# A tiled softmax whose stores alternate between the DMA queues of Pool and ACT

## The chip, the cores and the metric

The kernel runs on one core of a Trainium2 chip. The metric is the device time of one execution in microseconds; for several runs the median is given.

## The reference

The input `x` has the shape 32 x 512 x 1024 in float32, and `temperature` is 0.5. The output is a softmax over the last axis:

```python
scaled = x / temperature
shifted = scaled - np.max(scaled, axis=-1, keepdims=True)
exp_x = np.exp(shifted)
return (exp_x / np.sum(exp_x, axis=-1, keepdims=True)).astype(np.float32)
```

This is 16384 independent rows of 1024 numbers, 67.1 MB in and 67.1 MB out.

## The kernel before

The rows are cut into 11 tiles. A tile has 128 partitions, and each partition holds several whole rows: 11 in the first tile, 12 in tiles 1 to 9, and 9 in the last, tile 10. The rows of a partition are contiguous in memory, so that one DMA moves a whole tile with one contiguous run for each partition. Within a tile the rows are worked on in groups, which `PASSES` gives: 4, 4 and 3 rows in the first tile, 6 and 6 in the others, 4, 3 and 2 in the last.

Four buffers hold tiles (`BUFS`), and everything is done in place. SP issues the loads (line 62): four at the start, and then the load of tile i+4 after the store of tile i has landed, since it goes into the same buffer. For a group, `maximum` lets DVE reduce each row to its maximum (line 71) and scale it to a bias (line 74); `exponential` lets ACT take the exponential of each row with that bias, with the row's sum as a by-product (line 80); `divide` lets DVE take the reciprocal of the sums (line 92) and multiply the rows by it (line 95 in one instruction for tiles 2, 3, 4 and 6, line 98 row by row for the others). When the last group of a tile has been divided, `store` issues one DMA for the whole tile (line 110). The first store is held back by a small copy on Pool (line 108) that waits for the load of tile 2.

The order is written out by hand. Each engine runs its instructions in the order in which the loop emits them. For each group the loop emits the maximum and the exponential, and after these the divide (and, for a tile's last group, the store) of the group before it. From tile 9 on (`ALONE`) the last group of the tile before is finished ahead of the new tile's first maximum, and in the last tile (`HELD`) all three maxima and exponentials come ahead of the three divides. So on ACT a store stands in one line with the exponentials, and on Pool there is nothing but the stores and the small copy.

A store goes through the DMA queue of the engine that issues it: `queue = nc.gpsimd if i < BY_POOL else nc.scalar` with `BY_POOL = 6`. Tiles 0 to 5 are stored by Pool, tiles 6 to 10 by ACT. A transfer on a queue is served after those ahead of it on the same queue; transfers on different queues share the 16 DMA engines.

Of the kernel before, what the change touches and what calls it, by code (L numbers as in the profile page):

```python
# [1 line left out]

# [4 lines left out]

PASSES = [[4, 4, 3]] + [[6, 6]] * 9 + [[4, 3, 2]]  # L10
BUFS = 4

WHOLE = (2, 3, 4, 6)


BY_POOL = 6

ALONE = 9

HELD = len(PASSES) - 1  # L20


@with_exitstack
def kernel(
    ctx: ExitStack,
    tc: tile.TileContext,
    x: bass.AP,
    temperature: bass.AP,
    out: bass.AP,
):  # L30
    nc = tc.nc
    f32 = mybir.dt.float32
    scale = 1.0 / float(temperature)
    extreme = mybir.AluOpType.max if scale > 0 else mybir.AluOpType.min

    P = 128
    xf = x.flatten_outer_dims()
    of = out.flatten_outer_dims()
    n, d = xf.shape
    rows = [sum(ks) for ks in PASSES]  # L40
    assert sum(rows) * P == n

    data = ctx.enter_context(tc.tile_pool(name="data", bufs=BUFS))
    stats = ctx.enter_context(tc.tile_pool(name="stats", bufs=4))


    groups = []
    for i, ks in enumerate(PASSES):
        for j, k in enumerate(ks):
            groups.append((i, sum(ks[:j]), k))  # L50

    def dram(t, i):
        block = t[P * sum(rows[:i]) : P * sum(rows[: i + 1]), :]
        return block.rearrange("(p k) d -> p k d", p=P, k=rows[i])

    tiles, small = [], []

    def load():
        i = len(tiles)
        if i < len(PASSES):  # L60
            xt = data.tile([P, rows[i], d], f32, name="xt")
            nc.sync.dma_start(out=xt, in_=dram(xf, i))  # L62
            tiles.append(xt)

    def maximum(g):
        i, a, k = groups[g]
        top, bias, sums, recip = (
            stats.tile([P, k], f32, name=name) for name in ("top", "bias", "sums", "recip")
        )
        small.append((bias, sums, recip))  # L70
        nc.vector.tensor_reduce(  # L71
            out=top, in_=tiles[i][:, a : a + k, :], axis=mybir.AxisListType.X, op=extreme
        )
        nc.vector.tensor_scalar_mul(bias, in0=top, scalar1=-scale)  # L74

    def exponential(g):
        i, a, k = groups[g]
        bias, sums, _ = small[g]
        for b in range(k):
            nc.scalar.activation(  # L80
                tiles[i][:, a + b, :],
                tiles[i][:, a + b, :],
                mybir.ActivationFunctionType.Exp,
                bias=bias[:, b : b + 1],
                scale=scale,
                accum_out=sums[:, b : b + 1],
            )

    def divide(g):
        i, a, k = groups[g]  # L90
        _, sums, recip = small[g]
        nc.vector.reciprocal(recip, sums)  # L92
        if i in WHOLE:
            xt = tiles[i][:, a : a + k, :]
            nc.vector.tensor_mul(xt, xt, recip.unsqueeze(2).to_broadcast([P, k, d]))  # L95
            return
        for b in range(k):
            nc.vector.tensor_scalar_mul(  # L98
                tiles[i][:, a + b, :], in0=tiles[i][:, a + b, :], scalar1=recip[:, b : b + 1]
            )  # L100

    def store(g):
        i, a, k = groups[g]
        if a + k == rows[i]:
            if i == 0:


                nc.gpsimd.tensor_copy(stats.tile([P, 1], f32, name="seen"), tiles[2][:, 0, 0:1])  # L108
            queue = nc.gpsimd if i < BY_POOL else nc.scalar
            queue.dma_start(out=dram(of, i), in_=tiles[i])  # L110
            load()

    with tc.manual_schedule():
        for _ in range(BUFS):
            load()
        waiting = []

        def finish():  # L120
            for g in waiting:
                divide(g)
                store(g)
            waiting.clear()

        for g, (i, a, k) in enumerate(groups):
            if i >= ALONE and a == 0:
                finish()
            maximum(g)
            exponential(g)  # L130
            if i < HELD:
                finish()
            waiting.append(g)
        finish()


# [1 line left out]
_INS = ['x', 'temperature']  # L138
_OUTS = [((32, 512, 1024), 'float32')]

_NUMBERS = {'temperature': 0.5}


# [26 lines left out]
```

## Time and profile before

| what | value |
|---|---|
| time, median of 3 runs | 317.35 us (317.19 to 318.64) |
| the profiled execution: its time, its span | 318.96 us, 317.2 us |
| DVE busy | 252.3 us (80%) |
| ACT busy | 148.3 us (47%) |
| Pool busy | 3.7 us (1%) |
| moved | 134.24 MB, mean 423 GB/s |

The span runs from the first instruction to the last event that the profile shows; about 1.8 us of the profiled execution lie around it. In the profile, L110 is line 110 of the kernel; `xt<-in_x_dram` is a load, `out_dram<-xt` a store. Names such as SPq, POOLq and ACTq are the instruction queues of the engines, which issue the DMAs. DMA queue q1 is that of SP, q0 that of Pool (software_dynamic) and q10 that of ACT. A row of a timeline gives the start, the duration, the engine, the line and the operation, and in brackets the idle time before it with what ended it. A row of a table by stretch gives the stretch, its length, the busy time and count of DVE, ACT and Pool, the clock, the DMA's busy share and its GB/s.

### The profile page before, as it was taken

The page shows a single profiled execution, that of the slowest core. Times are in us where ns is not written, and L with a number is a line of the kernel's source. Part 1 is how long each engine was busy: PE and PEld are TensorE (multiplying, and loading weights), DVE is VectorE, ACT ScalarE, POOL GpSimd, SP SyncE. Part 2 cuts the span into 40 slices and gives each one's busy share as a digit, 9 for nine tenths or more (in the row PEclk, how much of TensorE's full clock was granted, in tenths as well). Part 3 has the DMA queues.
Part 4 walks back from the last instruction along what each step waited for, and adds up shares of the span by engine and source line. Part 5 has one row for each costly group of instructions (what it writes and reads, how often), then busy time and mean ns, then how long its engine had stood idle before and what let it go on. Part 6 is the DMA issues. An engine that isn't in the chain of part 4 may idle for free. (4 is left out here: it accounts for less than half of the span.)

```text
span 317.2 us, 542 instructions
## 1 busy us (share of the span) xinstructions
DVE 252.3 (80%) x160; ACT 148.3 (47%) x257; POOL 3.7 (1%) x11
## 2 busy tenths in 40 slices
DVE  0099999999999799969949994997199689779900
ACT  0048477468174353807171770438035805916600
POOL 0000010000000000000000000000000000000000
DMA  9999999999999999999999999999999999999994
GB/s 364 401 459 397 459 434 377 417 439 438 440 403 465 428 409 471 410 440 440 403 471 415 415 477 397 446 441 409 465 421 409 471 418 431 442 414 459 421 432 181
DMA packets 3171, 134.24 MB, mean 423 GB/s; under 512 B 352, under 2 KB 352, under 8 KB 352
## 3 DMA queue, kind: packets, MB, share of 16 engines
q1 hardware_dynamic: 1584, 67.11, 49.5%
q0 software_dynamic: 864, 37.22, 27.1%
q10 hardware_dynamic: 720, 29.88, 21.8%
q14 instruction: 3, 0.02, 0.0%
HBM read 67.11 MB, written 67.11 MB: 423 GB/s over the span
## 5 line engine op out<-in xcount | busy, mean ns | idle before, releaser
L80 ACT ACTIVATE xt<-xt,bias 128x1024 f32<-128x1024 f32 x128 | 145.2, 1135 | 133.7 <-DVE bias L74 64.6
L71 DVE TENSOR_REDUCE top<-xt 128x6 f32<-128x6144 f32 (+3 forms) x24 | 140.1, 5837 | 40.7 <-DMA xt<-in_x_dram 40.7
L98 DVE TENSOR_SCALAR xt<-xt,recip 128x1024 f32<-128x1024 f32 x80 | 54.5, 748 | 0.6
L95 DVE TENSOR_TENSOR xt<-xt,recip 128x6144 f32<-128x6144 f32 x8 | 52.5, 6559 | 0.6 <-DVE recip L92 0.2
L80 ACT ACTIVATION_READ_ACCUMULATOR xt<-xt,bias 128x1 f32 x128 | 23.8, 186 | 0.0
L80 ACT ACT_TABLE_LOAD x1 | 1.3, 1283 | 16.7 <-DMA xt<-in_x_dram 16.7
L92 DVE RECIPROCAL recip<-sums 128x6 f32<-128x6 f32 (+3 forms) x24 | 4.3, 180 | 5.8 <-ACT xt L80 5.8
L110 POOL DMA_DIRECT2D out_dram<-xt x6 | 3.3, 554 | 129.0 <-ACT xt L80 83.8
L74 DVE TENSOR_SCALAR bias<-top 128x6 f32<-128x6 f32 (+3 forms) x24 | 4.1, 171 | 0.8
L108 POOL COPY seen<-xt 128x1 f32<-128x1 f32 x1 | 0.2, 183 | 45.3 <-DMA xt<-in_x_dram 45.3
L151 POOL MEMSET const-bfloat16-1.0<- 128x1 bf16 x1 | 0.1, 102 | 0.0
L151 POOL MEMSET const-uint8-127<- 128x1 uint8 x1 | 0.1, 102 | 0.0
L151 POOL MEMSET const-float32-0.0<- 128x1 f32 x1 | 0.1, 99 | 0.2 <-issue 0.2
L151 POOL MEMSET const-float32-1.0<- 128x1 f32 x1 | 0.1, 99 | 0.0
## 6 DMA issues: line engine op xcount, KB each, us to landing
xt<-in_x_dram SPq DMA_DIRECT2D x9, 6144.0 KB, 37.1
out_dram<-xt POOLq DMA_DIRECT2D x5, 6144.0 KB, 36.7
out_dram<-xt ACTq DMA_DIRECT2D x4, 6144.0 KB, 32.6
xt<-in_x_dram SPq DMA_DIRECT2D x1, 5632.0 KB, 15.8
out_dram<-xt POOLq DMA_DIRECT2D x1, 5632.0 KB, 28.5
xt<-in_x_dram SPq DMA_DIRECT2D x1, 4608.0 KB, 39.5
out_dram<-xt ACTq DMA_DIRECT2D x1, 4608.0 KB, 15.5
```

Source lines behind the costliest of these rows:

```text
L71: nc.vector.tensor_reduce(out=top, in_=tiles[i][:, a : a + k, :], axis=mybir.AxisListType.X, op=extreme)
L74: nc.vector.tensor_scalar_mul(bias, in0=top, scalar1=-scale)
L80: nc.scalar.activation(tiles[i][:, a + b, :], tiles[i][:, a + b, :], mybir.ActivationFunctionType.Exp, bias=bias[:, b : b + 1], scale=scal ...
L92: nc.vector.reciprocal(recip, sums)
L95: nc.vector.tensor_mul(xt, xt, recip.unsqueeze(2).to_broadcast([P, k, d]))
L98: nc.vector.tensor_scalar_mul(tiles[i][:, a + b, :], in0=tiles[i][:, a + b, :], scalar1=recip[:, b : b + 1])
L108: nc.gpsimd.tensor_copy(stats.tile([P, 1], f32, name="seen"), tiles[2][:, 0, 0:1])
L110: queue.dma_start(out=dram(of, i), in_=tiles[i])
L151: nc = _bacc.Bacc("TRN2", target_bir_lowering=False, num_devices=1)
```

## The change

The rule for the queue of a store is no longer a limit but a list. Tiles 0, 2, 4, 6, 8 and 9 are stored by Pool, tiles 1, 3, 5, 7 and 10 by ACT. Pool still issues six stores and ACT five. On ACT each store keeps the place of its tile in the emitted order: the store of tile 1 now stands among ACT's exponentials after those of tile 2's first group, and so on. DVE and SP run the same instructions as before in the same order.

```diff
-BY_POOL = 6
+BY_POOL = (0, 2, 4, 6, 8, 9)
...
-            queue = nc.gpsimd if i < BY_POOL else nc.scalar
+            queue = nc.gpsimd if i in BY_POOL else nc.scalar
             queue.dma_start(out=dram(of, i), in_=tiles[i])
             load()
```

## The prediction

> **What bounds the kernel now.** I read the slices of the span and the DMA queues first, since they say whether any engine but the DMA has something to win.
>
> ```profile
> DMA  9999999999999999999999999999999999999994
> q1 hardware_dynamic: 1584, 67.11, 49.5%
> q0 software_dynamic: 864, 37.22, 27.1%
> q10 hardware_dynamic: 720, 29.88, 21.8%
> HBM read 67.11 MB, written 67.11 MB: 423 GB/s over the span
> ```
>
> The DMA engines are busy in every slice but the last. q1 carries the loads that SP issues, q0 the stores of Pool, q10 those of ACT; together they fill 98.4% of sixteen engines. A megabyte costs the same from each: 0.218 x 317.2 us / 29.88 MB = 2.31 us on q10, 2.31 us on q0, 2.34 us on q1. So a 12-row tile (6144 KB, 6.29 MB) costs all engines 14.55 us, and the last one (4608 KB, 4.72 MB) 10.9 us. q1's 1584 packets are 11 loads of 144, or 9 on each engine: 8 of data and one small one that ends the transfer. A data packet of a 12-row tile thus costs its engine 14.55/8 = 1.82 us, one of the last tile 1.36 us.
>
> The order of work at the end comes from the chain that ended last, from the stores on ACT's queue in the timeline, and from one row of DVE that shows when tile 9's load landed. I call the store and load of tile i S(i) and L(i).
>
> ```profile
> 208.96 35.04 DMA out_dram<-xt
> ...
> 244.14 39.52 DMA xt<-in_x_dram
> ...
> 283.68 4.43 DVE top L71
> ...
> 299.31 0.75 DVE xt L98
> ```
>
> ```profile
> 239.38 0.34 ACTq L110 DMA_DIRECT2D out_dram<-xt  x1
> 257.30 0.34 ACTq L110 DMA_DIRECT2D out_dram<-xt  x1
> 283.18 0.34 ACTq L110 DMA_DIRECT2D out_dram<-xt  x1
> 300.76 0.34 ACTq L110 DMA_DIRECT2D out_dram<-xt  x1
> ```
>
> ```profile
> 258.30 6.55 DVE L71 TENSOR_REDUCE top<-xt 128x6 f32<-128x6144 f32 x1 [1.02 <-DMA xt<-in_x_dram]
> ```
>
> S(6) lands at 244.0 and frees the buffer for L(10), which lands at 283.66. Then DVE and ACT need 17.1 us until S(10) is issued at 300.76. The DMA stays busy through these 17 us only because stores are still queued. How long they last, the DMA issues say when asked for the stretches around 239, 257, 283 and 300 us (KB and us from issue to landing):
>
> ```profile
> out_dram<-xt ACTq DMA_DIRECT2D x1, 6144.0 KB, 31.6
> out_dram<-xt ACTq DMA_DIRECT2D x1, 6144.0 KB, 33.6
> out_dram<-xt ACTq DMA_DIRECT2D x1, 6144.0 KB, 22.2
> out_dram<-xt ACTq DMA_DIRECT2D x1, 4608.0 KB, 15.5
> ```
>
> S(7) lands at 271.0, S(8) at 290.9, S(9) at 305.4, S(10) at 316.3; 0.9 us later the span ends. S(9) lasts 305.4 - 300.8 = 4.6 us beyond the issue of S(10). That is all the cover the tail has.
>
> Last, how two queues share the engines. Between 232 and 254 us both a load and a store were always queued:
>
> ```profile
> q1 hardware_dynamic: 109, 4.72, 49.7%
> q10 hardware_dynamic: 111, 4.67, 49.1%
> ```
>
> They take equal turns, packet by packet. This reproduces the tail by hand. L(10) lies behind L(9) until 258.3; its 8 packets alternate with 8 of stores: 8 x (1.36 + 1.82) = 25.4 us, landing 283.7 (measured 283.66). S(7) lands at 271.0, 12.7 us after 258.3, or four turns of 3.18 us: S(7) has four packets left at 258.3. S(8) gets the other four turns, and its last four packets alone take 7.3 us: 291.0 (measured 290.9). S(9) then takes 14.55 us: 305.5 (measured 305.4), S(10) 10.9 us: 316.3 (measured 316.3).
>
> **The change, part by part.** No arithmetic changes and no byte more is moved; 11 stores stay 11.
>
> *Issue.* S(1), S(3), S(5) go from Pool to ACT, S(6), S(8), S(9) from ACT to Pool, so ACT still issues five stores (0.34 us each, 0.85 the first) and Pool six (0.53). Behind a store on ACT stands the next group's exponential, which needs a maximum that DVE runs after the divide the store waits for (6.55 us and a 0.17 us bias). ACT's wait and its 0.34 us lie under that; without the cover three stores would cost 1 us in all. On Pool only later stores are queued. Pool is slower to start: the timeline has DVE's next maximum at 150.84, just after the last divide, and Pool's issue at 151.47, against 239.26 and 239.38 on ACT. So S(6), S(8), S(9) are issued some 0.7 us later, counting the longer issue; each then stands beside queued transfers, which hides it: nothing. S(10), the one that nothing covers, stays on ACT.
>
> *Bytes.* All queues pay 2.31 to 2.34 us per MB, so nothing is won or lost by moving bytes from one to the other.
>
> *Order of service.* Here is the cost. On one queue S(7) and S(8) are served one after the other, and a load beside them gets every second turn. On two queues both are served at once, and the load gets a smaller share. No row of this trace shows a store on q0, a store on q10 and a load all queued at length: at the handover, S(6) is issued on q10 at 208.96 while q0 finishes S(5). The bounds are every second turn (no slip) and every third. I take every third, because q1 and q10 share by equal turns above and q1 and q0 do so too (4.03 MB on q0 beside 3.83 MB on q1 from 188.5 to 206.5 us).
>
> Suppose everything up to 258.3 us stays: S(7) has four packets left, S(8) is queued. Four rounds of three, 4 x (1.82 + 1.82 + 1.36) = 20.0 us, end at 278.3; S(7) is done, S(8) and L(10) have four packets each. Four rounds of two, 12.7 us, end at 291.0, where L(10) lands and S(8) is done. L(10) lands 7.3 us later than before. Only S(9) is left to cover the 17.1 us of arithmetic: it ends at 305.5 while S(10) is issued at 291.0 + 17.1 = 308.1. The 2.6 us between, and the start of a transfer on idle engines, is time in which nothing moves. That start lies between nothing and 2.3 us (L(0) landed 15.8 us after its issue for 13.5 us of data); I take 1.2, the middle, since part of L(0)'s excess belongs to the first packets of the run. The end is 308.1 + 1.2 + 10.9 = 320.2, against 316.3: 3.9 us later. The profiled execution has a span of 317.2 us in a time of 318.96; its span becomes 321.1. The three runs shown have a median of 317.35, and I add the 3.9 to it: **321.2 us**.
>
> In general, each S(7) packet left when S(8) starts costs L(10) 1.82 us, and about 3.4 us (4.6 less the 1.2) are free: the loss begins at two packets, and four are there now.
>
> *Upstream.* The same overlap occurs at each earlier pair (S(0) lands some 9 us after S(1) is issued), so early stores land later and loads wait longer for buffers. But L(9) and L(10) are issued well before the queue ahead of them is empty (L(10) at 244.1 behind an L(9) that lands at 258.3), and some queue always has work, so the engines lose nothing there. It moves the phase: as stores win turns from loads, later stores come later against their predecessors. Whether S(7) meets S(8) with three, four or five packets left is the largest doubt: 1.8 us for each.
>
> *A rule against it.* The Trainium skill, DMA: Bandwidth & Descriptors, section Rules for kernel authors, says of spreading transfers over issuing engines for bandwidth: "Doesn't help — they all run on the same 16 DMA engines and interleave". By it alone the sum would be zero, 317.35 us; the equal price per MB above agrees with it on bandwidth, while the tail depends on which transfer comes first. The same page, section Queues, rings and completion order, has each engine take turns between queue rows packet by packet; by this the share would be a third, and the sum the one above, though no run here has shown three queues.
>
> **The rivals.**
>
> *No loss.* The load keeps half the turns, or S(7) is nearly done when S(8) starts, or the early engines decide. For the last there is a row, the end of the span:
>
> ```profile
> 313.00:317.20 4.20, 0.00 (x0) 0.00 (x0) 0.00 (x0) 1.00 0.06 26
> ```
>
> Only 6% of the engines' time is used after 313: most are done there, and one laggard ends at 316.3. The others have some 3 us less to do; if L(10) no longer waits for a packet of the laggard, it lands up to 3.4 us earlier than I reckon and the loss shrinks to about 0.5 us. Time: 317.3 to 318.4. Against it: the laggard serves the same packets as before.
>
> *Faster.* The laggard's 316.3 - 313 is the only DMA time left to win beside the start. If another order of packets spares it, the end comes up to 2.6 us earlier: 314.8 us. This decides only if the tail also keeps its cover, two packets or fewer of overlap; nothing in the profile says the laggard's lag comes from the queue chosen.
>
> *Worse.* S(9) is issued at about 283 and stands behind S(8) on q0. If S(8) ends two packets before L(10), S(9) spends two turns beside L(10) instead of under the arithmetic: 3.6 us more, about 324.8.
>
> **How the numbers follow.** About 0.5% (1.6 us) is what a measurement of this kernel can tell from no change. The forecast has 0.72 (its own span 319.2 to 323.4, one packet less to one packet more and the start latency), no loss 0.18, faster 0.05, worse 0.05. So slower by over 0.5% is 0.77, within 0.5% 0.18, faster 0.05. The range takes in the no-loss case and the forecast's upper end: 317.2 to 323.4.
>
> **What would show it.** Right: S(7)'s time to landing grows from 31.6 to about 39 us, L(10)'s from 39.5 to about 47; S(8) and L(10) land within a packet or two of each other; S(10) takes 12 to 13 us instead of 15.5; the DMA share falls near zero for some 3 us before S(10)'s data, where it is full now; q0 and q10 both carry data between 258 and 275. Wrong: L(10) landing near 284 with the share full to the end, or an idle stretch of the DMA in the middle.

## The result and the profile after

The changed kernel takes 325.16 us (median of 5 runs, 324.98 to 325.33), the kernel before 317.84 us (5 runs, 317.19 to 318.64). The ratio is 1.023, with a 95% interval from 1.021 to 1.0251: slower by 7.3 us, where 3.9 were forecast. The profiled execution of the changed kernel has a span of 323.4 us in a time of 325.16, so its span is 6.2 us longer than that of before. The granted clock was 1.00 in every run of this case, and the ratios leave out runs that lie over 1.5% above the fastest of their kernel.

The page of the changed kernel, its DMA slices and queues:

```profile
DMA  9999999998989999998989999999999999999666
q1 hardware_dynamic: 1584, 67.11, 48.8%
q0 software_dynamic: 864, 37.22, 27.1%
q10 hardware_dynamic: 720, 29.88, 21.4%
```

The bytes on each queue are the same. What is new is at the end: the last three slices are busy to between six and seven tenths. DVE and ACT are busy for 252.3 and 148.3 us as before.

The stores of tiles 7, 8, 9 and 10 in the timeline of ACT and Pool:

```profile
236.95 0.34 ACTq L110 DMA_DIRECT2D out_dram<-xt  x1
255.20 0.53 POOL L110 DMA_DIRECT2D out_dram<-xt  x1 [42.20 <-DVE xt L98]
281.92 0.53 POOL L110 DMA_DIRECT2D out_dram<-xt  x1 [26.18 <-DVE xt L98]
310.19 0.34 ACTq L110 DMA_DIRECT2D out_dram<-xt  x1
```

The DMA issues in the stretches around 237, 255, 282 and 310 us (KB, and us from issue to landing):

```profile
out_dram<-xt ACTq DMA_DIRECT2D x1, 6144.0 KB, 40.8
out_dram<-xt POOLq DMA_DIRECT2D x1, 6144.0 KB, 38.1
out_dram<-xt POOLq DMA_DIRECT2D x1, 6144.0 KB, 25.7
out_dram<-xt ACTq DMA_DIRECT2D x1, 4608.0 KB, 12.3
```

S(7) takes 40.8 us instead of 31.6 and lands at 277.7; S(8) lands at 293.3, S(9) at 307.6, S(10) at 322.5. The chain that ended last has the load of tile 10 and the first instruction that waits for it; DVE's timeline has the first of tile 9 (start, duration, and in brackets the idle time before it):

```profile
249.17 43.91 DMA xt<-in_x_dram
293.10 4.43 DVE top L71
```

```profile
256.77 6.55 DVE L71 TENSOR_REDUCE top<-xt 128x6 f32<-128x6144 f32 x1 [1.86 <-DMA xt<-in_x_dram]
```

L(9) lands 1.5 us earlier than before, L(10) 9.4 us later, at 293.08. Then follow 17.1 us of arithmetic until S(10) is issued. The table by stretch (busy time of DVE, ACT and Pool, the clock, the DMA's busy share, GB/s) shows the DMA in the second half of them. A packet counts whole in the stretch in which it starts, so a share can also exceed 1.

```profile
303.00:306.00 3.00, 2.93 (x7) 3.00 (x7) 0.00 (x0) 1.00 0.38 164
306.00:309.00 3.00, 2.93 (x7) 2.11 (x4) 0.00 (x0) 1.00 0.00 0
```

From 306 to 309 us no packet of data starts. In the trace's packets the last one of S(9), begun before 306, ends at 307.3 us, and the first of S(10) starts at 311.0: for 3.7 us nothing moves. The cover that S(9) gave the tail is used up before the arithmetic is done.

### The profile page after: what moved, and what is told of

Read it like the earlier page. It is cut to its first block, busy times and chain, and to the rows that moved or that the text cites. A ratio compares the mean times of both kernels' runs of the same rounds, so it can differ in the third digit from the quotient of the medians.

```text
span 323.4 us, 542 instructions
## 1 busy us (share of the span) xinstructions
DVE 252.3 (78%) x160; ACT 148.3 (46%) x257; POOL 3.7 (1%) x11
## 3 DMA queue, kind: packets, MB, share of 16 engines
q1 hardware_dynamic: 1584, 67.11, 48.8%
HBM read 67.11 MB, written 67.11 MB: 415 GB/s over the span
## 4 chain that ended last, share of the span: by engine, by line
DMA 65%; DVE 26%; ACT 5%; issue 0%; DVEq 0%; SPq 0%; ACTq 0%
DMA xt<-in_x_dram 43%; DMA out_dram<-xt 21%; DVE top L71 18%; DVE xt L98 5%; ACT xt L80 5%; DVE xt L95 2%; DVE bias L74 1%; DVE recip L92 0%; DVEq L165 0%; SPq L62 0%; ACTq L80 0%
## 6 DMA issues: line engine op xcount, KB each, us to landing
out_dram<-xt POOLq DMA_DIRECT2D x5, 6144.0 KB, 35.2
xt<-in_x_dram SPq DMA_DIRECT2D x1, 4608.0 KB, 43.9
out_dram<-xt ACTq DMA_DIRECT2D x1, 4608.0 KB, 12.3
```

## How the loss came about: turns taken from the last load

The step that no row of before could show is in this trace. From 262.5 to 272.5 us S(7) on q10, S(8) on q0 and L(10) on q1 were all queued (packets, MB, share of the engines):

```profile
q10 hardware_dynamic: 32, 1.57, 36.3%
q0 software_dynamic: 30, 1.47, 35.5%
q1 hardware_dynamic: 33, 1.22, 28.6%
```

The three queues take equal turns, about two packets each on each of the 16 engines. L(10) gets every third turn, where it had every second beside a single store queue.

Three theories were set against each other. Theory 1: the loss is this third turn, S(8) beside S(7), and the cover of the tail that it uses up. Theory 2: packets on Pool's queue are slow in the tail. Theory 3: the alternation among tiles 0 to 6 delays the loads.

**Holding S(8) back until S(7) has landed.**

```diff
             queue = nc.gpsimd if i in BY_POOL else nc.scalar
+            if i == 8:
+                nc.gpsimd.memset(tiles[7][:, 0, 0:1], 0.0)
             queue.dma_start(out=dram(of, i), in_=tiles[i])
```

> After's kernel with one more Pool instruction: before the store of tile 8 Pool writes one element of tile 7's buffer, which must wait until the store of tile 7 has landed (that buffer is not used again). So S(7) and S(8) are on two queues but no longer in flight together. Theory 1 (the loss is the third turn that S(8) takes beside S(7) and L(10)): L(10) lands near 284 us or earlier, its time to landing falls from 43.9 to below 40 us, the DMA stays full until the end, and the time returns to within 1.5 us of before, 316.5 to 319. Theory 2 (packets of stores on Pool's queue are slower at the end, whatever the overlap): some 2 us come back at most 4, time 321 to 323. Theory 3 (the alternation among the tiles 0 to 6 delays the loads): no change, 325.

Measured: 317.56 us against 317.38 for before, ratio 1.0009 (0.999 to 1.0029). All of the loss is gone, with S(8) still on Pool and the alternation still in place. S(8) is issued at 271.08 instead of 255.20. L(10) in the issues around 250 us, and the table by stretch during the last arithmetic:

```profile
xt<-in_x_dram SPq DMA_DIRECT2D x1, 4608.0 KB, 27.2
```

```profile
282.00:299.00 17.00, 16.79 (x19) 10.29 (x18) 0.53 (x1) 1.00 1.04 448
```

L(10) lands after 27.2 us instead of 43.9, and the DMA stays full. It keeps every second turn beside S(7), and from 270.4 us, when S(7) has landed, to 273.0, when the first packet of S(8) starts, it is alone. Theories 2 and 3, as they were stated, have no place for this.

**Delaying S(8) by part of the overlap.**

```diff
+            if i == 8:
+                idle = stats.tile([P, 256], f32, name="idle")
+                for _ in range(20):
+                    nc.gpsimd.tensor_copy(idle, tiles[8][:, 11, 0:256])
             queue.dma_start(out=dram(of, i), in_=tiles[i])
```

> The changed kernel with 20 small copies on Pool ahead of the store of tile 8 (they read one row of tile 8 after its divide and write a scratch tile), so that S(8) is issued some 6 to 9 us later but still before S(7) has landed. Theory 1: each round of three that S(8) misses, about 5 us, gives L(10) 1.82 us back: one and a half rounds, 2 to 4 us earlier, and 321 to 323.5, between the changed kernel and the one that holds S(8) back until S(7) has landed. Theory 2: the packets on Pool's queue stay as slow, 324.5 to 325.5.

Measured: 318.17 us against 317.72, ratio 0.9999 (0.9971 to 1.0028); 3 to 5 us more came back than theory 1 had allowed, and theory 2 does not fit at all. S(8) is issued at 264.01, 8.8 us later than in the changed kernel. What that sum had left out is the time from the issue to the first packet. The DMA queues from 264 to 268 us, and then from 268 to 270 us:

```profile
q1 hardware_dynamic: 25, 0.92, 53.3%
q10 hardware_dynamic: 23, 0.79, 45.5%
```

```profile
q0 software_dynamic: 16, 0.79, 90.8%
q1 hardware_dynamic: 5, 0.18, 21.3%
q10 hardware_dynamic: 9, 0.00, 0.3%
```

S(8)'s first packet, one on each engine, starts between 268.1 and 269.5 us, over 4 us after the issue, and by 269.4 S(7) has landed. So there was no overlap left, and this run repeats the one before it: it is no test of a partial overlap. L(10), issued at 249.2:

```profile
xt<-in_x_dram SPq DMA_DIRECT2D x1, 4608.0 KB, 34.7
```

It lands at 283.9, within 0.3 us of before, and the cover holds.

**Alternating up to tile 7, then ACT alone.**

```diff
-BY_POOL = (0, 2, 4, 6, 8, 9)
+BY_POOL = (0, 2, 4, 6)
```

> After's kernel with tiles 8 and 9 back on ACT: the stores alternate up to tile 7, and S(7) to S(10) share ACT's queue. Theory 1: S(7) and S(8) are served one after the other, the tail is that of before, 317 to 319. Theory 2: no Pool store is left in the tail, also 317 to 319. Theory 3: the loss came earlier and stays, 323 to 325.

Measured: 318.01 us against 317.38, ratio 1.003 (1.0005 to 1.0054). The whole early alternation costs at most half a per cent. L(10), issued at 249.4, takes 35.2 us. Theory 3 falls.

**Changing the queue of tiles 8 and 9 alone.**

```diff
-BY_POOL = (0, 2, 4, 6, 8, 9)
+BY_POOL = (0, 1, 2, 3, 4, 5, 8, 9)
```

> Before's queues for tiles 0 to 7 and 10, after's for 8 and 9: Pool stores 0 to 5, 8 and 9, ACT 6, 7 and 10. The queue changes within the tail alone. Theory 1: S(7) has about four packets left when S(8) starts, L(10) slips by about 7 us, and the time is 320 to 325. Theory 2: slow packets of S(8) and S(9) beside L(10) as in the changed kernel, about 2 us, 319.5 to 320.5. Theory 3: the early part is that of before, 317 to 318.5.

Measured: 325.25, 326.66, 327.13 and once 319.47 us. Even the shortest is 2.1 us above before's 317.38; with times this far apart no ratio is given. The tail alone brings the loss, but by two very different amounts for one kernel. In the trace of the run with 325.25 us fifteen engines have finished L(10) by 287.3 us, and the sixteenth at 293.1. DVE waits for the last of them: L(10) counts as landed at 293.08, as in the changed kernel, and the span (323.5 us) is the same. Had it counted from the fifteen, the run would be 5.8 us shorter, 319.5 us, which is what the fourth run took. That the fourth run had no laggard is inferred: there is no trace of it.

**The overlap with the queues exchanged.** This takes the limit of before and raises it, so that S(7) is on Pool's queue and S(8) on ACT's.

```diff
-BY_POOL = 6
+BY_POOL = 8
```

> Before's kernel with the limit at 8: Pool stores tiles 0 to 7, ACT 8, 9 and 10. Now S(7) is on Pool's queue and S(8) on ACT's, so they overlap as in the changed kernel with the queues exchanged. Theory 1: L(10) again loses turns and the time is 320 to 324; without slow packets of Pool's S(8) beside L(10) it is some 2 us below the changed kernel. Theory 2 (Pool's queue in the tail is what costs): at most half of the loss, 317.5 to 319. Theory 3: 317 to 318.5.

Measured: 319.41 us against 317.38, ratio 1.0054 (1.0025 to 1.0083), between the ranges of theories 1 and 2. The trace shows the overlap of theory 1: the same stretch, 262.5 to 272.5 us, has the same equal turns:

```profile
q0 software_dynamic: 32, 1.57, 36.3%
q10 hardware_dynamic: 32, 1.57, 36.3%
q1 hardware_dynamic: 32, 1.18, 27.5%
```

L(10) lands 41.9 us after its issue at 246.0, at 287.9. Here no engine lags: all sixteen finish L(10) between 286.2 and 287.9. This is the smallest loss seen with the full overlap, 2.0 us, and S(7)'s packets on Pool's queue are not slow.

**Strict alternation to the end, and the mirror image.** The first puts S(9) on ACT's queue and S(10) on Pool's; the second has tiles 1, 3, 5, 7 on Pool and all others on ACT.

```diff
-BY_POOL = (0, 2, 4, 6, 8, 9)
+BY_POOL = (0, 2, 4, 6, 8, 10)
...
-BY_POOL = (0, 2, 4, 6, 8, 9)
+BY_POOL = (1, 3, 5, 7)
```

> Strict alternation to the end: Pool 0, 2, 4, 6, 8, 10, ACT 1, 3, 5, 7, 9; against the changed kernel only tiles 9 and 10 change queues. S(8) is on Pool's queue and S(9) on ACT's, so S(9), issued at about 282, no longer stands behind S(8) but takes a third turn beside S(8) and L(10). Theory 1: three more turns of 1.82 us go to stores ahead of L(10), it lands near 298, and less of S(9) is left to cover the arithmetic: some 5 to 6 us slower than the changed kernel, 329 to 332. Theory 2 (Pool's queue is what costs in the tail): S(9) leaves Pool's queue, so equal or up to 2 us faster, 323 to 325.

> The alternation with the queues exchanged and the last three stores on ACT: Pool 1, 3, 5, 7, ACT 0, 2, 4, 6, 8, 9, 10. S(7) is on Pool's queue, S(8) and S(9) on ACT's; the loads and the overlaps are those of the changed kernel. Theory 1: the loss is that of the overlap, whichever queue holds which store: 322 to 326. If the slow packets of the tail (2.1 to 2.8 us instead of 1.82) belong to Pool's S(8) beside L(10), they are gone here and the time is 321 to 323; if they belong to the three streams, they show again and it is 324 to 326.

Measured: strict 329.05 us (four runs, 326.18 to 333.17) against 317.72, ratio of the runs compared 1.0307 (1.0233 to 1.038); mirror 329.5 us (328.48 to 332.94) against 317.58, ratio 1.0378 (1.0298 to 1.0458). The strict version's time is as theory 1 expected, though not in the way expected: ten engines finish L(10) by 286.7 us, before S(9) reaches them, and only lagging ones serve S(9) beside it; the last finishes at 300.2. The mirror is above the expected range: its last engine finishes L(10) at 300.5, while twelve have done so by 286.7. There the lag is older than the tail: the engines had already finished the load of tile 8 at anything from 218.7 to 230.0 us. Both traces are of the longest run of their kernel (333.17 and 332.94 us).

One table ties these runs together (us, from the profiled execution of each). The sixteen engines finish L(10) one by one; the table gives the middle of their times (the mean of the eighth and the ninth) and the last, at which L(10) counts as landed. The second trace of the changed kernel is that of the run at the end of this section.

| kernel | L(10), middle engine | L(10) landed | S(10) issued | span | span less L(10) landed |
|---|---|---|---|---|---|
| before | 279.2 | 283.7 | 300.8 | 317.2 | 33.5 |
| S(8) held back | 273.7 | 277.9 | 299.4 | 316.8 | 39.0 |
| S(8) delayed | 281.0 | 283.9 | 301.0 | 316.1 | 32.2 |
| alternating up to tile 7 | 279.2 | 284.7 | 301.8 | 318.5 | 33.9 |
| limit 8 | 286.6 | 287.9 | 305.0 | 318.3 | 30.4 |
| changed | 290.5 | 293.1 | 310.2 | 323.4 | 30.3 |
| changed, second trace | 286.4 | 294.6 | 311.7 | 324.9 | 30.3 |
| tiles 8, 9 alone | 286.5 | 293.1 | 310.2 | 323.5 | 30.4 |
| strict | 286.7 | 300.2 | 317.6 | 331.4 | 31.2 |
| mirror | 284.8 | 300.5 | 317.6 | 331.2 | 30.7 |

In the first four, without the overlap of S(7) and S(8), the DMA has work to the end, and the last store waits in line. In the others the cover is gone, and the span is the landing of L(10) on its last engine plus some 30.3 us (31.2 at most): arithmetic, S(10), and the end. So once the cover is gone the size of the loss is decided by one number, and that by the slowest of sixteen engines.

The loss therefore has two parts. The third turn moves the middle engine by the same 7.3 us in four of the six traces that have it, from 279.2 to about 286.5, and costs some 2 us of time where no engine lags (limit 8). The rest, about 5 of the 7.3 us in the changed kernel, comes with engines that finish L(10) later still. No run here took the lag away and kept S(8) on Pool's queue beside S(7) and L(10), except perhaps the run of 319.47 us, so what makes engines lag in this overlap is not shown.

**The queues by themselves.** All stores on ACT, then all on Pool, and the first once more:

```diff
-BY_POOL = (0, 2, 4, 6, 8, 9)
+BY_POOL = ()
...
-BY_POOL = (0, 2, 4, 6, 8, 9)
+BY_POOL = tuple(range(11))
```

> All eleven stores on ACT's queue. Theory 1: one queue serves the stores in order as before, nothing overlaps, 317 to 318.5, the same as before. If the choice of the queue itself has a price (descriptors made by Pool, a cost for each MB), the time moves by over 1 us from before, to the faster side if Pool's is the dearer one.

> All eleven stores on Pool's queue. Theory 1: no overlap between stores, 317 to 318.5, plus up to 0.7 us for Pool's later issue of the last store. If bytes on Pool's queue are dearer than on ACT's, the time is above 319.

> All stores on ACT's queue once more, for a trace of one of its longer runs (they went from 317.9 to 323.9 us, where the first trace is of 317.9). If one engine lags, L(10) is spread over 4 us or more between the first and the last engine; if the queue is slower, its MB cost over 2.35 us. Theory 1 expects the first, 317 to 324.

Measured: Pool alone 317.97 us against 317.58, ratio 1.0003 (0.9974 to 1.0031). ACT alone 320.77 us against 317.72 (ten runs, 317.91 to 323.92), ratio 1.0072 (1.0032 to 1.0112), above what I expected; again 321.68 and 323.5, ratio 1.0142 (1.0057 to 1.0228), from two runs. By itself Pool's queue is thus not the dear one. The trace of the 321.68 us run says that ACT's is not dear either (its queue line, and the ends by stretch):

```profile
q10 hardware_dynamic: 1584, 67.11, 48.5%
```

```profile
313.00:316.00 3.00, 0.00 (x0) 0.00 (x0) 0.00 (x0) 1.00 0.11 49
316.00:319.90 3.90, 0.00 (x0) 0.00 (x0) 0.00 (x0) 1.00 0.02 9
```

A megabyte costs 0.485 x 319.9 / 67.11 = 2.31 us, as in the kernel before. But after 313 us almost all engines are done, and one goes on to 319: L(10) lands on it at 282.7, on the first at 276.7. So it is a laggard again, by 6 us, with no store on Pool and all stores on one queue. Why all stores on ACT have one more often than all on Pool is not explained.

**The changed kernel once more.** This run has no edit; it asks whether the first trace was typical.

> The changed kernel once more, for its trace. In the first trace of it data packets of the tail took longer than 1.82 us (some 2.2 us more in all for each engine between 260 and 290 us). If this belongs to the order of transfers, L(10) lands again near 293 us (some 2 us beyond the forecast of 291.0), and the time is 325. If it was chance, the time falls to 322 to 323.5 in this run.

Measured: 326.63 us for the profiled execution, 324.89 for the other; before 317.72, ratio 1.0233 (1.0154 to 1.0313), from two runs. L(10) landed at 294.6. Ten engines finished it by 287.1 us, six between 291.5 and 294.6; in the first trace all sixteen did so between 289.1 and 293.1. The late landing repeats; how many engines are late varies.

## Why the prediction was right in kind and wrong in size

*What bounds the kernel, and the issue.* Right. The DMA engines bound it, and moving the stores between engines cost little by itself: nothing measurable with all on Pool, 0.7% with all on ACT. The price per megabyte held too: 2.31 us for q0 when Pool stores everything (0.491 x 316.1 / 67.11).

*Four rounds of three, 20.0 us, to 278.3.* The turns are equal, as forecast, and S(7) landed at 277.7. But thirteen of the sixteen engines had finished it by 274.5, and S(7) had been issued 2.4 us earlier than before, so that the end agrees to 0.6 us is partly luck.

*Four rounds of two, 12.7 us, to 291.0.* This is the step that failed, by its size. From 277.7 to the landings of L(10) and S(8) at 293.1 and 293.3 it took 15.4 us and more, and 294.6 was L(10)'s landing in the second trace. The slip of 7.3 us itself is what the middle engine shows in the table (7.2 in the second trace). The forecast, though, set out from the slowest engine of before (283.7, over 4 us behind the middle one), and took its lag and the price of a packet, 1.82 or 1.36 us, to stay the same beside other transfers. Neither did. Between 274 and 288 us the changed kernel has:

```profile
DMA packets 122, 5.06 MB, mean 362 GB/s; under 512 B 3, under 2 KB 3, under 8 KB 3
...
q0 software_dynamic: 55, 2.70, 54.4%
q1 hardware_dynamic: 64, 2.36, 42.6%
```

A megabyte of S(8) costs 0.544 x 14 / 2.70 = 2.82 us there instead of 2.31, one of L(10) 2.53 us. On 2.70 and 2.36 MB that is 1.4 + 0.5 = 1.9 us. The missing 2.1 us are of that size, but this is a mean over all engines beside the landing on the slowest, so the sum only makes it plausible. In the second trace q0 pays 0.713 x 14 / 3.98 = 2.51 in the same stretch. With the limit at 8 the whole tail, from 258 to 296 us, has

```profile
q10 hardware_dynamic: 216, 9.83, 59.7%
q1 hardware_dynamic: 112, 3.54, 21.6%
q0 software_dynamic: 80, 3.15, 19.1%
```

A megabyte there costs 2.30 to 2.32 us on each queue. So the slow packets are no necessary part of the overlap. In the mirror they appear again, this time in what is left of S(7) on Pool's queue (0.54 MB at 3.2 us from 268 to 280 us), while q10 beside it pays 2.33. They come with late engines and are slowest on q0: in the mirror beside two busy queues, in the changed kernel mostly after S(7) is done, with only L(10) beside. But q0 and q1 also share the engines when Pool stores everything, at 2.31 us. What makes the packets slow stays open.

*Upstream.* Right that little is lost there. S(6) landed at 249.0 us instead of 244.0 and L(10) was issued 5.0 us later, but it still stood behind L(9); with the alternation up to tile 7 alone the time rose by at most half a per cent.

*The arithmetic and the last store.* Right: 17.1 us, then 12.3 where 12.1 were forecast, so the start of a transfer on idle engines costs about 1.4 us. The DMA stood still for 3.7 us, where 2.6 + 1.2 = 3.8 were forecast.

*The base.* The second part of the miss. The span was forecast as 321.1 and came out at 323.4, 2.3 us more. The time was forecast as 321.2 and came out at 325.16, 4.0 us more. The other 1.7 us is that I added a difference of spans to the median of 317.35, although the profiled execution of before, at 318.96, stood 1.6 us above it. That execution has a laggard ending at 316.3; other runs of before have spans from 315.0 us. In the changed kernel S(10) starts on all idle engines at once, so a lag before it does not add to the end a second time. The difference should have been taken from an end without the laggard, or the profiled execution's own time kept as the base throughout.

*The rivals.* "No loss" had the right warning, the laggard, but on the wrong side: I had used it only as a reason why the loss might be smaller. The table shows that it is also why the loss is larger: 287.9 on the last engine gave a span of 318.3 us, 293.1 one of 323.5. "Worse" did not occur in the changed kernel, where S(8) and L(10) land 0.2 us apart.

## What to carry to other kernels

Where the DMA bounds a kernel as it does this one, queues decide the order in which transfers finish, even where they do not change the rate: a load that the end waits for loses turns to every store that is in flight on another queue beside it. Keep such stores behind each other on one queue, or hold the next one back, and count in packets how many turns of overlap the work behind the last load can bear. Reckon the landing for the slowest engine, since a transfer has landed only when all sixteen have finished it.

## What was unexpected in the hardware

Transfers that cost 2.31 to 2.34 us for a megabyte over the whole of the kernel before became slower in the tail of the changed kernel. From 282 to 290 us, where DVE and ACT do nothing at all and Pool only issues one store, q0 still pays 0.608 x 8 / 1.87 = 2.60 us, and all engines together move 381 GB/s; so the arithmetic's use of the memory is no explanation for this part. And in the first trace the first store that ACT issues (S(1), at 66.16 us) held ACT's queue for 4.37 us, against 0.85 us for the first one in before and 0.34 for the later ones; ACT's exponentials ran on beside it. In the second trace of the same kernel it was 1.18 us, and with all stores on ACT the first took 0.37; the cause is not known.
